# Differential attention: the two score products in turn on the two row halves of the array, and a mask that VectorE writes

## The chip, the cores and the metric

The kernel runs on one core of a Trainium2 chip. The metric is device time in microseconds of one execution, the median of three runs. Four compute engines matter here: TensorE multiplies matrices (PE in the profile; its weight loads are listed apart, as PEld), VectorE (DVE) and ScalarE (ACT) work on elements, GpSimd (POOL) does small things. DMAs bring the weights from memory.

## The reference, cut to what matters

The reference is a network of two layers and a last block, on 256 tokens of width 1024. A layer is a feed-forward part, a mixer and another feed-forward part. The mixer has three branches, and one of them is differential attention with 8 heads. A head has two sets of queries and keys of 64 features each; each set gives a softmax, and the second one times a learned lambda is subtracted from the first:

```python
sc = jnp.einsum('bqhmd,bkhmd->bhmqk', qblk, k).astype(jnp.float32) * scale   # m: the two parts
allowed = kchunk[None, :] <= (qp // CHUNK)[:, None]                          # chunks of 64 keys
p = jax.nn.softmax(jnp.where(allowed, sc, -jnp.inf), axis=-1)
w = p[:, :, 0] - lam_full * p[:, :, 1]
```

A query sees the keys of its own chunk of 64 and of the earlier ones. With query blocks of 128 that leaves one forbidden square in each block: the first 64 queries of a block against the last 64 of the keys that the block looks at.

## The kernel before, in words

All activations stay on the chip, and the weights (some 420 MB) stream through it once. A weight tile of 512 KB is loaded, split by ScalarE and VectorE into a high and a low part (`split`, lines 257 and 258), and multiplied as three products (lines 252 to 254, and 295 to 298). A list of items holds the weight tiles in order. After each tile, every active chain of other work (attention, state space and so on) is advanced by one stage, so the short products of the chains stand between the long streams of the weight products. The queues of the engines are in order; a scheduler at build time sets the order of the instructions and puts in the semaphores.

The chain of differential attention is `diff`. It is a software pipeline over the 8 heads with four stages: `s1` makes scores and softmax of a head, `s2` transposes the weights `p`, `s3` multiplies by the values, `s4` transposes the outputs. One step of the pipeline runs `s1` of head h, `s4` of h - 3, `s2` of h - 1 and `s3` of h - 2, in this order, and then waits for two weight tiles. There are 8 heads in each of two layers, so `s1` runs 16 times.

In `s1` the queries and keys of part m lie on partitions 64 m to 64 m + 63, so part 0 uses the upper half of the array's rows and part 1 the lower half. For each part, one PSUM bank `x[m]` takes the scores of both query blocks: columns 0 to 127 for block 0, columns 128 to 383 for block 1. Each score product (lines 753 and 755) is in float32, which runs as two passes. Behind each stands a product of one row in bf16 (lines 754 and 756) that adds a row with -1e30 in its first 64 entries, so that the first 64 queries lose the last 64 keys. VectorE then takes the maxima (757 and 758) and scales them (759), ScalarE the exponentials with their sums (763 and 765), VectorE the reciprocals, and the two parts are joined into `p` (771 and 772).

The array is used in three shapes around `s1`: all 128 rows in the weight products and transposes, 64 rows in the score products, and one row in the mask products.

Of the kernel before, what the change touches and what calls it, by code (L numbers as in the profile page):

```python
# [26 lines left out]
# order of the weight tiles and of the chains of work in the mixer and in the second block  # L27
# [3 lines left out]
# chains whose instructions come first where there is a choice  # L31
PRIO = {'narrow': 300, 'rope2': 300}
# leading weight tiles that are split ahead, in scratch of the chains
SPARE, SPARE2 = (1, 2), (1,)
# steps of the substitution that other work may follow
# [3 lines left out]
# 2 pi in parts of 8 bits (and a rest), so that products with 16-bit counts are exact  # L39
# [8 lines left out]
NEG = -1.0e30  # L48

# column offsets of the segments of w_mix_in  # L50
C_QA, C_KA, C_VA, C_Z, C_XBC, C_DT, C_QC, C_KC, C_VC, C_G = (
    0, 1024, 2048, 3072, 4096, 5632, 5648, 6672, 7696, 8720)
# column offsets in the table of constants
# [26 lines left out]
# [128, a, b] in tiles of 512 columns  # L80
# [9 lines left out]
class Net:  # L90
# [31 lines left out]
    # the constants that the first matrix products don't need  # L122
    def setup1(self):
        nc, I, T = self.nc, self.I, self.ctab
        nc.sync.dma_start(T[:, 128:384], I["ctab"][:, 128:384])
        T2 = self.t8([128, 1, 640], F32, "ctab2")[:, 0, :]
# [6 lines left out]
        nc.vector.tensor_copy(B[:, 128:384], T2[:, 384:640])  # L133
        nc.vector.tensor_copy(B[:, 384:512], T[:, 0:128])
        self.m_str, self.m_cau, self.m_chk, self.identb = (B[:, o:o + 128] for o in (0, 128, 256, 384))
# [3 lines left out]
        self.oneb = B[0:1, 512:576]  # L139
        nc.vector.memset(self.oneb, 1.0)  # L140
# [25 lines left out]
    # scratch of a chain; `prv` for scratch of the evacuation of projections  # L166
# [17 lines left out]
    # ---- order of work: a list of weight tiles and of things to do; chains advance one stage per weight tile  # L184
# [45 lines left out]
    # weight block [128, a, b] -> exact split into hi + lo  # L230
    def wload(self, src, a, b, spare=False):
        n = a * b
# [5 lines left out]
        if spare:  # L238
            # in scratch of the chains
            hi, lo = ([self.s2.tile([128, 512], F32R, name=i, tag="sc") for _ in range(2)] for i in ("hi", "lo"))  # L240
            for i in range(2):
                self.split(hi[i], lo[i], raw[:, i * 512:i * 512 + 512])
            return Rows(hi, b), Rows(lo, b)
# [5 lines left out]
    # three exact products hi*hi + hi*lo + lo*hi  # L249
# [19 lines left out]
    # the same for several columns: scalar engine, and one step of Newton's  # L269
# [17 lines left out]
    # ys[n] += (a^T)[tokens]^T @ W ; stationary a^T, moving W  # L287
# [13 lines left out]
    # [128 tok, n] per token block; fn(ps0, ps1)  # L301
# [32 lines left out]
    # [128 f, 2, 256 tok] of 256 columns; fn(ps)  # L334
# [21 lines left out]
    # 16 columns, token-major [128 tok, 2, 16] for the chain fn(pd)  # L356
# [20 lines left out]
    # token-major output of 1024 columns over kt tiles of a^T; the last tiles block by block; fn(tb, ys)  # L377
# [35 lines left out]
    # residual, layer norm, transposition: new x, x^T  # L413
# [40 lines left out]
    # one token block of x^T as hi, lo [128, 8, 256]  # L454
# [12 lines left out]
    def ffn(self, S_, w_in, w_out, g, b, mod=False, first=False):  # L467
# [12 lines left out]
        # first 256 columns token-major, so that they can start on the first token block  # L480
# [74 lines left out]
    # vectors of a layer, as columns or on every partition  # L555
    def columns(self, l, L):
# [29 lines left out]
        # lambda of the differential attention  # L586
# [128 lines left out]
    # rotary embedding of 4 heads (two parts each) and transposition  # L715
# [26 lines left out]
    # differential attention, one head a stage  # L742
    def diff(self, L):
# [3 lines left out]
        def s1(h):  # L747
            qT, kT = L["qa"], L["ka"]
            x = [self.bank([128, 384]) for _ in range(2)]
            mx = self.small.tile([128, 4], F32, name="mx", tag="mx")  # L750
            for m in range(2):
                p = slice(64 * m, 64 * m + 64)
                nc.tensor.matmul(x[m][:, 128:384], qT[p, h, 128:256], kT[p, h, :], start=True, stop=False)
                nc.tensor.matmul(x[m][:, 320:384], self.m_chk[0:1, :], self.oneb, start=False, stop=True)
                nc.tensor.matmul(x[m][:, 0:128], qT[p, h, 0:128], kT[p, h, 0:128], start=True, stop=False)
                nc.tensor.matmul(x[m][:, 64:128], self.m_chk[0:1, :], self.oneb, start=False, stop=True)
                nc.vector.tensor_reduce(mx[:, m:m + 1], x[m][:, 0:128], axis=AX.X, op=ALU.max)
                nc.vector.tensor_reduce(mx[:, 2 + m:3 + m], x[m][:, 128:384], axis=AX.X, op=ALU.max)
# [49 lines left out]
    # stages of n items, in a software pipeline; `rest` weight tiles for each step  # L808
# [10 lines left out]
    # softplus of a small [128, n] tile, accurate to float32 for small results too  # L819
# [18 lines left out]
    # step sizes and cumulated decays of the state-space branch  # L838
    def steps(self, L, pd):
# [21 lines left out]
        # the cumulated decays of every head as rows, hi and lo (first, second, second block)  # L861
# [7 lines left out]
    # causal convolution and twice the silu of 256 channels  # L869
# [93 lines left out]
    # stick-breaking attention, two heads of one parity a stage  # L963
    def stick(self, L):
# [5 lines left out]
        def s1(t):  # L970
# [11 lines left out]
            for nm, z in (("B", flat(B)), ("A", flat(A))):  # L982
# [3 lines left out]
                if t == 0 and nm == "B":  # L986
                    # one table for both exp and ln
                    self.tc.keep_in_program_order(nc.scalar.preload_act_table_set("natural_log_exp_and_others"))
# [48 lines left out]
    # vectors of the second block  # L1037
# [35 lines left out]
    # gain * cos and gain * sin of the rotary angles of the given positions, for q and k  # L1073
# [35 lines left out]
    # adaptive modulation: shift, gain, gate (twice) as rows of a DRAM tile  # L1109
    def modulation(self):  # L1110
# [3 lines left out]
        for s in range(6):  # L1114
# [11 lines left out]
            # sums over the partitions, as rows: quarter j on the partitions from 32 j  # L1126
# [20 lines left out]
    # two rows of the modulation on every partition  # L1147
# [7 lines left out]
    # modulated rms norm of one token block; out(n): where half n goes  # L1155
# [23 lines left out]
    def block2(self, S_, us):  # L1179
# [14 lines left out]
        # hi and lo of the two halves of the merged heads, transposed  # L1194
# [53 lines left out]
    # causal convolution and twice the silu of 256 channels  # L1248
# [15 lines left out]
    # decays and step sizes of the delta rule  # L1264
# [29 lines left out]
    # sums of squares over the heads of [128 f, 4, 256 tok], as [128 tok, 2, 8]  # L1294
# [12 lines left out]
    # queries, attention (transposed) and values of the delta rule  # L1307
    def gdn_qv(self, B):
# [5 lines left out]
        # what the squared norms of the queries make of the constant in the norm of the outputs  # L1314
# [25 lines left out]
    def gdn(self, B):  # L1340
# [4 lines left out]
        # values times step size, and decayed keys of the first chunk  # L1345
# [7 lines left out]
        # inverse norms of the keys  # L1353
# [23 lines left out]
        # decay, M (transposed) and attention (transposed); index tb * 8 + parity * 4 + i, head 2 i + parity  # L1377
# [28 lines left out]
    def chunk0(self, B, Xt):  # L1406
# [4 lines left out]
        # chunk 0  # L1411
# [18 lines left out]
    # outputs of one chunk, and their transposes  # L1430
# [62 lines left out]
    # transposed inverses of the 16 unit lower triangular I + M: blocks of 16 by substitution, one in each  # L1493
    # partition; then by doubling the block size
    def inverse(self, B, MT, Xt):
# [9 lines left out]
        # [(g, b, j), i, x, m] = M_m[i, j] of block (g, b) where x = b, transposed to [(g, x, m), i, b, j]  # L1505
# [11 lines left out]
        # Z[c, j] = inverse[j, c]  # L1517
# [28 lines left out]
        # levels and quarters, those of the first chunk ahead  # L1546
# [10 lines left out]
        # the last level needs just the quarter of M below the diagonal  # L1557
# [41 lines left out]
        # the inverses themselves; of the last level's input only the first quarter  # L1599
# [19 lines left out]
    # rotated heads of one token block, normalized unless the inverse norms (times 1 / 8) are to go to `out`  # L1619
# [103 lines left out]
    # gate, residual and modulated norm of the second half; then the experts  # L1723
    def gated(self, S_, B):
# [7 lines left out]
        def head():  # L1732
            # the router takes x: its weights times the gain, and the products of the shift
# [13 lines left out]
        def fn(tb, ys):  # L1747
# [19 lines left out]
            # column 8 p + k goes to k, p  # L1767
# [9 lines left out]
    # weights of an expert: gate and up for rows 8 p + k as [128, k, 2, 256], down for rows 2 p + k as [128, k, 1024]  # L1777
# [29 lines left out]
    # the same for the expert with the rows `idx`; beyond the last row nothing is read  # L1807
# [17 lines left out]
    # tokens of one block as hi + lo  # L1825
# [9 lines left out]
    # choice of experts: combine weights, places in the experts' slots and in the extra units  # L1835
    def route(self, B):
# [13 lines left out]
        # per token block and group  # L1850
# [4 lines left out]
        # one-hots of the first maximum and of the second among the 8 of every group; of the first group  # L1855
# [37 lines left out]
        # one-hots over all experts, and their places: rank among the expert's tokens, 0 where there is none  # L1893
# [17 lines left out]
        # weights of both choices  # L1911
# [16 lines left out]
        # units beyond the first 64 tokens of an expert  # L1928
        def rest():
# [14 lines left out]
            # which expert a unit belongs to; 32 where none  # L1944
# [360 lines left out]
```

## Time and profile before

| | |
|---|---|
| median of 3 runs | 2203.24 us (2202.16 to 2209.62) |
| span of the profiled execution | 2200.1 us (no other time of that execution is listed; the timed runs lie 2.1 us and more above it) |
| TensorE busy | 2142.3 us, 97% of the span |
| VectorE, ScalarE busy | 1346.7 us (61%), 994.9 us (45%) |
| DMA | 428.93 MB, 195 GB/s in the mean |
| the 16 runs of `s1` | 365 to 453 us (layer 0), 1219 to 1305 us (layer 1) |

Times in the rows are microseconds from the start of the span. A matrix product's row begins with its start; its end is modelled, so what the engine can do is read from one start to the next. A product that waits for its weights is listed from the start of the load. In a timeline, neighbouring instructions of one line are merged into one row with a count, and the second number is the time from the first start to the last end.

### The profile page before, as it was taken

To read this page: it belongs to the slowest core of one execution; us is meant where nothing else is said; L and a number is where in the kernel's file an instruction comes from. 1 tells how busy PE (TensorE), PEld (TensorE's weight loads), DVE (VectorE), ACT (ScalarE), POOL (GpSimd) and SP (SyncE) were. 2 spreads that over 40 slices of the span, in tenths; PEclk is the share of its full clock that TensorE was granted. 3 is DMA by queue.
4 is the path that set the end of the run, shared out by engine and by line. 5 is a ranking of instruction groups with operands and counts; after the bars stand their busy time and mean duration, and the time that the engine had idled before them with its cause. 6 is when DMAs were issued, how large, how long until landed. Compare 5 with 4: busy or idle time off the path is not lost.

```text
span 2200.1 us, 35342 instructions
## 1 busy us (share of the span) xinstructions
PE 2142.3 (97%) x14123; PEld 1821.5 (83%) x14123; DVE 1346.7 (61%) x2258; ACT 994.9 (45%) x1671; POOL 83.0 (4%) x73
## 2 busy tenths in 40 slices
PE   8999999999999999999999999999999899799998
PEld 8997987899999987998888789998998788544543
DVE  5556567765676667666677775567554895732232
ACT  5443554664554443444465565544443555211111
POOL 0000000100000000000000010000000021101000
PEclk9999999999999999999999999999999999899999
DMA  7665534444466786888543345555666423799996
GB/s 237 182 209 174 172 108 115 134 140 150 148 201 220 233 267 210 265 271 262 169 135 107 115 126 153 154 171 175 187 219 189 131 81 111 263 344 330 357 340 244
DMA packets 316984, 428.93 MB, mean 195 GB/s; under 512 B 20782, under 2 KB 262672, under 8 KB 315792
## 3 DMA queue, kind: packets, MB, share of 16 engines
q1 hardware_dynamic: 316384, 423.48, 61.5%
q8 instruction: 113, 1.85, 0.4%
q0 software_dynamic: 432, 3.15, 0.3%
q14 instruction: 55, 0.45, 0.1%
HBM read 425.50 MB, written 1.07 MB: 194 GB/s over the span
## 4 chain that ended last, share of the span: by engine, by line
PE 86%; DVE 6%; DMA 4%; ACT 1%; issue 1%; POOL 0%; SPq 0%; DVEq 0%; ACTq 0%; POOLq 0%
PE ps L252 14%; PE ps L254 14%; PE ps L253 14%; PE ps L1983 5%; PE y L295 4%; PE y L296 4%; PE ps L295 3%; PE ps L298 3%; PE ps L296 3%; PE y L298 3%; PE ps L2025 3%; DMA raw<-in_w_ada_dram 3%; PE y L284 1%; PE y L2038 1%; DVE lo L258 1%; PE ps L2130 1%
## 5 line engine op out<-in xcount | busy, mean ns | idle before, releaser
L258 DVE TENSOR_TENSOR lo<-raw,hi 128x1024 fp32r<-128x1024 f32 (+1 forms) x556 | 662.2, 1196 | 442.3 <-ACT hi L257 439.8
L257 ACT CAST hi<-raw 128x1024 fp32r<-128x1024 f32 (+1 forms) x556 | 568.8, 1028 | 711.2 <-PE ps L253 264.8
L254 PE MATMUL ps<-xh,lo 128*128 128x256 f32 (+1 forms) x2232 | 633.3, 284 | 3.5 <-DVE lo L258 3.5
L252 PE MATMUL ps<-xh,hi 128*128 128x256 f32 (+1 forms) x2232 | 636.6, 285 | 0.0
L253 PE MATMUL ps<-xl,hi 128*128 128x256 f32 (+1 forms) x2232 | 633.2, 284 | 0.0
L254 PEld LDWEIGHTS ps<-xh,lo 128*128 128x128 f32 (+1 forms) x2232 | 427.3, 191 | 4.4 <-DVE lo L258 3.7
L252 PEld LDWEIGHTS ps<-xh,hi 128*128 128x128 f32 (+1 forms) x2232 | 427.5, 192 | 2.4 <-issue 1.6
L253 PEld LDWEIGHTS ps<-xl,hi 128*128 128x128 f32 (+1 forms) x2232 | 427.4, 192 | 0.6
L295 PE MATMUL ps<-hi,xh 128*128 128x512 f32 (+1 forms) x368 | 147.1, 401 | 1.2 <-ACT xh L257 0.7
L298 PE MATMUL ps<-hi,xl 128*128 128x512 f32 (+1 forms) x368 | 144.6, 393 | 0.8 <-DVE xl L258 0.6
L296 PE MATMUL ps<-lo,xh 128*128 128x512 f32 (+1 forms) x368 | 144.2, 392 | 0.0
L295 PE MATMUL y<-hi,hh 128*128 128x512 f32 x352 | 137.5, 391 | 0.0
L296 PE MATMUL y<-lo,hh 128*128 128x512 f32 x352 | 137.0, 389 | 0.0
L1983 PE MATMUL ps<-wgu,hi 128*64 128x512 f32 x512 | 125.2, 601 | 0.0
L298 PE MATMUL y<-hi,hl 128*128 128x512 f32 x352 | 104.6, 389 | 0.0
L1983 PEld LDWEIGHTS ps<-wgu,hi 128*64 128x64 f32 x512 | 42.6, 139 | 71.0 <-issue 68.6
L1124 DVE SCALAR_TENSOR_TENSOR macc<-raw,cols,macc 128x1024 f32<-128x1024 f32 x42 | 53.9, 1284 | 57.0 <-DMA raw<-in_w_ada_dram 56.7
L295 PEld LDWEIGHTS ps<-hi,xh 128*128 128x128 f32 x368 | 70.5, 191 | 17.7 <-issue 2.0
L298 PEld LDWEIGHTS ps<-hi,xl 128*128 128x128 f32 x368 | 70.2, 191 | 17.2 <-DVE xl L258 2.7
L296 PEld LDWEIGHTS ps<-lo,xh 128*128 128x128 f32 x368 | 70.2, 191 | 13.1
L295 PEld LDWEIGHTS y<-hi,hh 128*128 128x128 f32 x352 | 66.1, 188 | 14.2 <-issue 0.8
L298 PEld LDWEIGHTS y<-hi,hl 128*128 128x128 f32 x352 | 66.1, 188 | 13.8
(607 smaller groups left out, 3248.7 us busy)
## 6 DMA issues: line engine op xcount, KB each, us to landing
raw<-in_w_mix_in_dram SPq DMA_DIRECT2D x184, 512.0 KB
raw<-in_ffn_w_in_dram SPq DMA_DIRECT2D x176, 512.0 KB
raw<-in_ffn_w_out_dram SPq DMA_DIRECT2D x88, 512.0 KB
wgu<-in_w_gate_dram SPq DMA_DIRECT2D x64, 512.0 KB
wgu<-in_w_up_dram SPq DMA_DIRECT2D x64, 512.0 KB
lo<-in_w_down_dram SPq DMA_DIRECT2D x54, 512.0 KB
raw<-in_w_branch_dram SPq DMA_DIRECT2D x48, 512.0 KB
raw<-in_w_ada_dram SPq DMA_DIRECT2D x48, 512.0 KB
```

The source lines that it names most:

```text
L252: mm(out, ah, bh, start=start, stop=False)
L253: mm(out, ah, bl, start=False, stop=False)
L254: mm(out, al, bh, start=False, stop=stop)
L257: self.nc.scalar.copy(hi, src)
L258: self.nc.vector.tensor_tensor(lo, src, hi.bitcast(F32), op=ALU.subtract)
L284: self.nc.tensor.transpose(pt[:, k, :], src[:, k * 128:(k + 1) * 128], self.ident)
L295: mm(y, ah[:, t], wh[:, c], start=start, stop=False)
L296: mm(y, ah[:, t], wl[:, c], start=False, stop=False)
L298: mm(y, al[:, t], wh[:, c], start=False, stop=stop)
L1124: nc.vector.scalar_tensor_tensor(acc, raw, c, acc, op0=ALU.mult, op1=ALU.add)
L1983: mm(gu[64 * e:64 * e + 64, c], u["x"](k)[:, 64 * e:64 * e + 64], w, start=k == 0 and i == 0, stop=k == KD - 1 and i == len(ws[0]) - 1)
L2025: mm(y[64 * e:64 * e + 64, :], u["hT"][:, k, 64 * e:64 * e + 64], wd[k][:, c], start=k == 0, stop=k == 1)
```

## The change

Both score products of query block 1 come first, part 0 and then part 1, and then both of block 0. The four mask products are gone. In their place VectorE writes -1e30 into the forbidden squares of each bank, both squares in one instruction (64 partitions, 2 x 64 columns), after the products and before the maxima. The bank's view grows from 384 to 512 columns so that the two squares lie at one stride (a bank holds 512 in any case). The table of constants loses the mask's row and its row of ones.

```diff
-            x = [self.bank([128, 384]) for _ in range(2)]
+            x = [self.bank([128, 512]) for _ in range(2)]
             mx = self.small.tile([128, 4], F32, name="mx", tag="mx")
+
+            for c, t, n in ((128, slice(128, 256), 256), (0, slice(0, 128), 128)):
+                for m in range(2):
+                    p = slice(64 * m, 64 * m + 64)
+                    nc.tensor.matmul(x[m][:, c:c + n], qT[p, h, t], kT[p, h, 0:n], start=True, stop=True)
             for m in range(2):
-                p = slice(64 * m, 64 * m + 64)
-                nc.tensor.matmul(x[m][:, 128:384], qT[p, h, 128:256], kT[p, h, :], start=True, stop=False)
-                nc.tensor.matmul(x[m][:, 320:384], self.m_chk[0:1, :], self.oneb, start=False, stop=True)
-                nc.tensor.matmul(x[m][:, 0:128], qT[p, h, 0:128], kT[p, h, 0:128], start=True, stop=False)
-                nc.tensor.matmul(x[m][:, 64:128], self.m_chk[0:1, :], self.oneb, start=False, stop=True)
+
+                nc.vector.memset(x[m][0:64, :].rearrange("p (a b) -> p a b", a=2)[:, :, 64:128], NEG)
                 nc.vector.tensor_reduce(mx[:, m:m + 1], x[m][:, 0:128], axis=AX.X, op=ALU.max)
                 nc.vector.tensor_reduce(mx[:, 2 + m:3 + m], x[m][:, 128:384], axis=AX.X, op=ALU.max)
...
-        nc.vector.tensor_copy(B[:, 128:384], T2[:, 384:640])
+        nc.vector.tensor_copy(B[:, 128:256], T2[:, 384:512])
...
-        self.oneb = B[0:1, 512:576]
-        nc.vector.memset(self.oneb, 1.0)
```

## Rows read from the trace of the kernel before

**Rows 1.** The page: busy times, and the chain that ended last.
```profile
PE 2142.3 (97%) x14123; PEld 1821.5 (83%) x14123; DVE 1346.7 (61%) x2258; ACT 994.9 (45%) x1671; POOL 83.0 (4%) x73
...
PE 86%; DVE 6%; DMA 4%; ACT 1%; issue 1%; POOL 0%; SPq 0%; DVEq 0%; ACTq 0%; POOLq 0%
```

**Rows 2.** Busy time by stretch: length, engines with counts, granted clock, DMA share, GB/s.
```profile
365.00:453.00 88.00, 88.00 (x547) 73.04 (x546) 68.23 (x172) 54.22 (x142) 7.68 (x6) 1.00 0.41 120
...
1219.00:1305.00 86.00, 86.00 (x487) 70.56 (x486) 62.18 (x155) 48.10 (x123) 6.14 (x5) 0.94 0.40 117
```

**Rows 3.** Timeline of PE around the first and last `s1`; count of one mask line.
```profile
365.20 0.70 PE L753 MATMUL y<-ka,qa 64*128 64x256 f32 x2
365.83 0.20 PE L754 MATMUL y<-bmask 1*128 1x64 bf16 x1
365.96 0.48 PE L755 MATMUL y<-ka,qa 64*128 64x128 f32 x2
366.37 0.20 PE L756 MATMUL y<-bmask 1*128 1x64 bf16 x1
366.50 0.70 PE L753 MATMUL y<-ka,qa 64*128 64x256 f32 x2
...
367.80 0.50 PE L296 MATMUL ps<-lo,xh 128*128 128x512 f32 x1
...
1301.03 0.70 PE L753 MATMUL y<-ka,qa 64*128 64x256 f32 x2
...
1303.63 0.44 PE L284 MATMUL y<-ctab,oa 128*128 128x128 f32 x2
...
L756 PE MATMUL y<-bmask x32: 197/198/198, 366.4 to 1303.5; 1*128 1x64 bf16 x32
```

**Rows 4.** Timeline of PE: products of 64 rows that stay on one half.
```profile
1772.02 1.16 PE L1392 MATMUL y<-gkk 64*128 64x128 f32 x8
1773.10 0.38 PE L1388 MATMUL y<-ctab,gg 128*128 128x128 f32 x1
...
245.10 0.71 PE L977 MATMUL y<-qc,kc 64*128 64x128 f32 x4
245.65 1.03 PE L980 MATMUL y<-qc,kc 64*128 64x256 f32 x4
246.61 0.28 PE L981 MATMUL y<-bmask 128*128 128x256 bf16 x1
```

**Rows 5.** Timeline of PE: line 1327 takes one half and then the other.
```profile
1805.15 0.70 PE L1678 MATMUL y<-sqkT 64*128 64x256 f32 x2
1805.69 1.60 PE L1327 MATMUL y<-gqv,gkk 64*128 64x128 f32 x16
1807.22 0.50 PE L296 MATMUL ps<-lo,xh 128*128 128x512 f32 x1
```

**Rows 6.** Groups of VectorE by form: busy, mean ns, idle before.
```profile
L559 DVE MEMSET rows<- 128x128 f32 x2 | 0.3, 165 | 0.0
L757 DVE TENSOR_REDUCE mx<-y 128x1 f32<-128x128 f32 x32 | 9.3, 291 | 14.3 <-PE y L756 14.1
```

**Rows 7.** Waits in 360 to 453: us, times, longest.
```profile
ACT hi L257 <- PE ps L253: 7.9, 8, 1.5
```

**Rows 8.** Timeline of VectorE and PE: head 2 of layer 0, then head 7.
```profile
391.43 0.75 DVE L772 SCALAR_TENSOR_TENSOR p<-p,sm 128x128 f32<-128x128 f32 x2
...
395.05 0.49 PE L284 MATMUL y<-ctab,p 128*128 128x128 f32 x3
...
450.45 0.74 DVE L772 SCALAR_TENSOR_TENSOR p<-p,sm 128x128 f32<-128x128 f32 x2
...
451.53 0.49 PE L284 MATMUL y<-ctab,p 128*128 128x128 f32 x3
```

**Rows 9.** Low clock in layer 1, one stretch of three, behind PE's row ahead.
```profile
1230.30 0.20 PE L756 MATMUL y<-bmask 1*128 1x64 bf16 x1
...
1231.05:1234.45 3.40, 3.40 (x19) 3.40 (x17) 0.87 (x3) 1.46 (x7) 0.00 (x0) 0.50 0.28 98
```

More of the change, by code (lines that the diff above doesn't have):

```diff
@@ L132, in setup1 @@
         nc.vector.tensor_copy(B[:, 0:128], T2[:, 256:384])
-        nc.vector.tensor_copy(B[:, 128:384], T2[:, 384:640])
+        nc.vector.tensor_copy(B[:, 128:256], T2[:, 384:512])
         nc.vector.tensor_copy(B[:, 384:512], T[:, 0:128])
-        self.m_str, self.m_cau, self.m_chk, self.identb = (B[:, o:o + 128] for o in (0, 128, 256, 384))
+        self.m_str, self.m_cau, self.identb = (B[:, o:o + 128] for o in (0, 128, 384))
         nc.vector.tensor_copy(B[:, 576:704], self.U)
```

## The prediction

> **What bounds the kernel now.** I read the page first: TensorE is busy for 97% of the span, and 86% of the chain that ended last is its work [rows 1]. A busy share can hide waits, so next the busy times by stretch, for the two stretches in which `s1` runs: TensorE is busy for all 88.00 of 88.00 us and all 86.00 of 86.00 us there, DMA for 0.41 of its time, ScalarE for 54 us, VectorE for 68 us [rows 2]. There the path is TensorE's queue itself; what is taken out of it ends the run sooner, as long as the products behind it have their inputs. The engine to watch is VectorE, at 68.23 of 88 us.
>
> Then the timeline of the score products. One head's `s1` begins at 365.20 and the next product at 367.80, so it holds the queue for 2.60 us; the last one holds it from 1301.03 to 1303.63, the same, and 32 mask products of line 756, two to a head, make 16 heads [rows 3]: 41.6 us in all. From start to start, a part is 0.63 us for the two passes of 256 columns (365.20 to 365.83), 0.13 for a mask product, 0.41 for the two passes of 128, 0.13 for a mask product; and the same again for part 1.
>
> **What a pass and a change of shape cost.** Line 1392 makes eight passes of 64 rows and 128 columns on one half in a row: 1772.02 to 1773.10, 1.08 us [rows 4]. Two of them alone take 0.41. Six passes more cost 0.67, so a pass of 128 columns costs u = 0.112 us, and entering and leaving such a run costs 0.41 - 0.22 = 0.19 us: a first load that nothing hides, and the wait at the end before a product of another shape. The pair of 256 columns gives v = (0.63 - 0.19)/2 = 0.22 for a pass. A check: line 977 and line 980, four passes of each width without a change between, should take 0.19 + 0.45 + 0.87 = 1.51; they take 245.10 to 246.61, 1.51 [rows 4]. So a head before is four passes of 256 and four of 128 (1.32 us), four times 0.19 (0.76), and four mask products (0.52): 2.60.
>
> **The change, step by step.**
>
> *The mask products go, and with them the changes of shape.* Four times 0.13 goes, and of four entries and exits one stays, 3 x 0.19 = 0.57. Left is 1.32 + 0.19 = 1.51 us if the passes still run one after the other: 1.09 less a head, 17.4 us over 16.
>
> *The halves take turns.* Does a pass on the lower half run beside one on the upper? Line 1327 does both halves in turn, eight passes on one and eight on the other. With line 1678 ahead of it, 18 passes run from 1805.15 to 1807.22, 2.07 us [rows 5]; one after another they would take 0.19 + 0.44 + 16 x 0.112 = 2.42. So 0.35 us, three passes, ran beside others. The second half begins when three passes of the first are still to come, and then both stream at full rate. In the new order a half never has more than two passes before the other half's turn, so here the two halves can run beside each other nearly throughout: half of 1.32, and 0.19, which is 0.85 us; if the lower half starts one load later (the 0.19 less an exit of some 0.08), 0.96. I take the middle, 0.90: 1.70 less a head, 27.2 us over 16. The ends are 1.51 (nothing side by side) and 0.85.
>
> The Trainium skill has a rule that speaks against this: "TensorE: Matmul & The Clock Gate", in the section on packing small matmuls ("The mechanism"), says that products start and end strictly in program order. By that rule a head would take 1.07 us and 24.5 us would be saved in all. The rows speak against it: strict order could hide one pass of line 1327 at the change of halves, and three are hidden [rows 5].
>
> *VectorE's two writes a head.* The trace has no write of a constant into PSUM. From below, the 128 x 128 MEMSET in SBUF takes 165 ns; from above, the maximum over 128 columns of the same bank, 291 ns [rows 6]. I take 0.2 us, nearer to the first, since the operation is the same: 32 x 0.2 = 6.4 us of VectorE's time, 3.2 in each stretch (2.6 to 4.7). By itself it lies beside the weight products that TensorE has queued behind the scores. The instruction waits for the products in its bank, as the maximum did; behind it in VectorE's queue stand the maxima and the splits of weights. The splits have room: ScalarE's half of the split waited 8 times for the weight products to give their buffers back [rows 7], so it runs as far ahead as the buffers let it.
>
> *The chain from maxima to `p`.* It must be over when the next step transposes `p`. For head 2, VectorE ends `p` at 391.43 + 0.75 = 392.18 and the transposes start at 395.05, 2.9 us later; for head 7, the last, it ends at 451.19 and they start at 451.53, 0.3 us later [rows 8]. Between a head's start and its transposes lie two runs of `s1`, so the transposes come 3.4 us sooner (1.7 for the last head). The chain gains too: both banks are complete about 1 us after the head's start, where part 1 took 2.6, less 0.4 for the two writes: about 1.2 us. The room falls from 2.9 to 2.9 - 3.4 + 1.2 = 0.7 us, and for the last head from 0.3 to about -0.2. And VectorE has 68 + 3 = 71 us of work in a stretch that shrinks from 88 to 74. So some of the gain comes back as waits for `p`: I put 0.2 us on each of 15 steps, 3 us (0 to 10).
>
> *The clock.* In layer 1 the granted clock is 0.94 over the stretch [rows 2], from three pieces of 3.4 us at half the full clock (1.2 in place of 2.4 GHz). The first begins at 1231.05, 0.6 us after the last mask product of an `s1` group (1230.30 and 0.13 for the product) [rows 9], and the other two follow such a group alike; layer 0, with the same groups, has none. Such a piece costs half its length, 1.7 us, 5.1 together. The new group has less dead time, so I expect two of the three to go, 3.4 us; other pieces may come or go as everything moves. Ends: 0 and 5.1.
>
> *The smaller constants* are made while the first layer streams, and cost nothing that ends late.
>
> **The sum.** The profiled span is 2200.1 us, and the median of the timed runs is 3.1 above it; I carry that over. -27.2 (products) + 3.0 (waits for `p`) - 3.4 (clock) = -27.6: a span of 2172.5, and a time of 2175.6 us.
>
> **The rivals.**
>
> *The halves don't overlap.* The 64-row passes run in series, without drains. For it: the overlap is shown for passes of 128 columns only, and at one change of halves. Against it: nothing else distinguishes the passes. -17.4 - 3.4 + 1 = -20, 2183 us.
>
> *The passes keep their order.* If a pass never starts before the one ahead of it in the program, only neighbours of different halves run together: three widths of 0.22 and two of 0.112 in series, and 0.19, is 1.07 us; 16 x 1.53 = 24.5 less, and 2203.2 - 24.5 - 3.4 + 3.0 = 2178 us. (This is the skill's rule above.) The three hidden passes speak against it.
>
> *VectorE takes over in the two stretches.* 71 of 74 us leaves it no room for its own waits. For it: in-order queues and 0.7 us of room for `p`. Against it: weight splits are far ahead, and the busy time counts an overlap of neighbours. If 10 us come back, 2203.2 - 27.2 - 3.4 + 13 = 2186 us.
>
> *Each change of halves costs like a change of shape.* Then all four pairs keep their 0.19 and only the masks go: 0.52 x 16 = 8.3 us, 2195 us. Rows 5 argue against it.
>
> *The change does nothing for the time:* what leaves the queue returns as waits; 2203 us. A queue without a gap speaks against it.
>
> *Slower: the write into PSUM is dear.* One mechanism: a write of 64 partitions in two pieces that takes VectorE 2 us and not 0.2. VectorE then needs 68 + 16 x 2 = 100 us in a stretch of 88, TensorE waits for `p` in every step, and each layer loses about 8 to 12 us net of what its own waits left free: about 2219 us. It decides from (88 - 68)/16 = 1.2 us a write on. Against it stand 165 and 291 ns [rows 6].
>
> **How the numbers follow.** Overlap with most of the gain kept: 0.57, 2176 us, by itself from 2169 to 2182. Kept order: 0.05. Series: 0.13. VectorE takes over: 0.14. Drains at each change: 0.05. Nothing: 0.02. Slower: 0.04. A measurement of this kernel tells about 0.3%, 6.6 us, from no change; so faster is the first four and part of the fifth, 0.91; same 0.05; slower 0.04. The range is 2167 to 2190: its lower end is 0.85 us a head, all three clock pieces gone, no waits (-28 - 5.1 is 2170) and 3 us for clock pieces elsewhere; the upper end takes in the cases at 2178, 2183 and 2186 with 4 us to spare.
>
> **What would show it.** In the profile after, one head from its first score product to the next other product: 0.85 to 0.96 us if the halves overlap, 1.5 if they run in series, 2.1 if each change drains. MEMSET rows on the score banks near 0.2 us. In the waits of TensorE, transposes of `p` waiting for line 772's successor: some tenths at most on a step; more than 0.7 on each would be VectorE taking over. The granted clock in layer 1's stretch above 0.94. A head of 1.07 us would show the kept order. The prediction is wrong if a head takes over 1.2 us or if TensorE's idle time in the two stretches passes 8 us.

## The result, and the profile after

| | before | after |
|---|---|---|
| median of the timed runs | 2202.7 us (2201.84 to 2209.62, 4 runs) | 2175.21 us (2174.6 to 2176.39, 4 runs) |
| span of the profiled execution | 2200.1 us | 2173.1 us (its own time 2174.99) |
| TensorE busy | 2142.3 us | 2113.4 us |
| VectorE busy | 1346.7 us | 1342.6 us |

The ratio is 0.9876, with a 95% interval of 0.9855 to 0.9897: the kernel became faster, by 27.5 us in the medians. The forecast was 2175.6 us.

The first two lines of the page after, busy times and the chain, answer to [rows 1]. TensorE is still what bounds the kernel, with the same share of a shorter span.

```profile
PE 2113.4 (97%) x14059; PEld 1805.8 (83%) x14059; DVE 1342.6 (62%) x2289; ACT 994.7 (46%) x1671; POOL 83.3 (4%) x73
...
PE 85%; DVE 7%; DMA 4%; ACT 2%; issue 1%; POOL 0%; SPq 0%; ACTq 0%; DVEq 0%; POOLq 0%
```

The busy times of the two stretches after, in the columns of [rows 2]. The stretch of layer 0 is 75 us long where it was 88, that of layer 1 about 73 where it was 86. TensorE's queue now has 1.3 us of gaps in each. VectorE has 65 of 75 us, and the granted clock of layer 1 is 1.00 where it was 0.94.

```profile
365.00:440.00 75.00, 73.69 (x506) 65.15 (x505) 65.29 (x181) 50.46 (x133) 8.19 (x6) 1.00 0.47 141
1206.00:1279.20 73.20, 71.89 (x492) 63.39 (x491) 64.30 (x178) 48.80 (x129) 6.98 (x6) 1.00 0.48 144
```

TensorE's timeline after, the first two runs of `s1`, answers to [rows 3]. The eight passes of a head are now one row, since nothing stands between them. From their start to that of the next product it is 366.30 - 365.44 = 0.86 us, where it was 2.60. The second head has the one gap of its layer that follows a group at once: 373.28 - 371.76 = 1.52 us, of which the bracket shows 0.60 of waiting for `p`.

```profile
365.44 0.92 PE L753 MATMUL y<-ka,qa 64*128 64x256 f32 x8
366.30 0.50 PE L294 MATMUL ps<-lo,xh 128*128 128x512 f32 x1
...
371.76 0.92 PE L753 MATMUL y<-ka,qa 64*128 64x256 f32 x8
373.28 0.30 PE L282 MATMUL y<-ctab,p 128*128 128x128 f32 x1 [0.60 <-DVE p L772]
```

VectorE's groups by form after, answering to [rows 6]: busy time, mean ns, idle before. The write into PSUM takes 165 ns, as the MEMSET in SBUF did, and the maxima behind it 277 ns.

```profile
L757 DVE TENSOR_REDUCE mx<-y 128x1 f32<-128x128 f32 x32 | 8.9, 277 | 0.0
L756 DVE MEMSET y<- 64x128 f32 x32 | 5.1, 165 | 1.3 <-PE y L753 0.8
```

TensorE's waits for `p` in the whole run after (us, times, longest; line 282 is line 284 of before, the transposes); the list of before has no such row.

```profile
PE y L282 <- DVE p L772: 2.6, 4, 0.7
```

**A measure for one stretch.** Total times of variants differ by a few us in parts of the run that no edit touches: the granted clock falls for pieces of 3.4 us and more at places that shift. So I also compare traces by place. Each product that no edit touches is paired with its like (same tiles and shape, same count from the start) in the first profile of before, and the median difference of start times is taken just ahead of a stretch (330 to 360 us, 1190 to 1215 us on the clock of before) and just behind it (490 to 500, 1330 to 1340). What it grows by is what the stretch gained or lost. The group sum is the time of the 16 runs of `s1` in TensorE's queue, from the first pass to the next product that is not a score or mask product; a wait at its end counts in it (1.2 of the 15.0 us after, so 13.8 without).

| kernel | group sum, us | layer 0, us | layer 1, us | time, us (ratio, 95% interval) |
|---|---|---|---|---|
| before | 41.68 | 0 | 0 | 2202.7 |
| before, second profile | 41.68 | +1.6 | -3.3 | 2202.27 (0.998 to 1.0011) |
| after | 15.0 | -11.5 | -16.2 | 2175.21 (0.9855 to 0.9897) |
| after, second profile | 15.0 | -11.5 | -16.2 | 2177.96 (0.9873 to 0.9911) |
| part by part | 15.1 | -12.0 | -16.7 | 2177.28 (0.9866 to 0.9898) |
| mask products kept | 22.8 | -9.4 | -14.1 | 2178.06 (0.9869 to 0.9901) |
| one half | 24.1 | -7.7 | -12.5 | 2174.7 (0.9864 to 0.99) |
| no mask | 13.7 | -11.7 | -16.4 | 2173.35 (0.9852 to 0.9885) |
| two writes | 20.0 | -9.2 | -13.6 | 2178.96 (0.9879 to 0.9912) |
| six writes | 24.5 | +2.3 | -3.4 | 2202.57 (0.998 to 1.0005) |
| late transposes | 15.0 | -12.3 | -17.0 | 2170.11 (0.9823 to 0.9875) |

(The ratio is to the kernel before on the same chip, whose medians lay between 2200.78 and 2203.11 us.) The two profiles of after agree to 0.1 us in both stretches. By the intervals, none of the variants from "part by part" to "two writes" can be told from the change itself; by the stretches they can.

### The profile page after: what moved, and what is told of

Its sections match the earlier page's. It is cut to its first block, busy times and chain, and to the rows that moved or that the text cites. A ratio compares the mean times of both kernels' runs of the same rounds, so it can differ in the third digit from the quotient of the medians.

```text
span 2173.1 us, 35223 instructions
## 1 busy us (share of the span) xinstructions
PE 2113.4 (97%) x14059; PEld 1805.8 (83%) x14059; DVE 1342.6 (62%) x2289; ACT 994.7 (46%) x1671; POOL 83.3 (4%) x73
## 3 DMA queue, kind: packets, MB, share of 16 engines
HBM read 425.50 MB, written 1.07 MB: 196 GB/s over the span
## 4 chain that ended last, share of the span: by engine, by line
PE 85%; DVE 7%; DMA 4%; ACT 2%; issue 1%; POOL 0%; SPq 0%; ACTq 0%; DVEq 0%; POOLq 0%
PE ps L250 14%; PE ps L252 14%; PE ps L251 14%; PE ps L1983 5%; PE y L293 4%; PE y L294 4%; PE ps L293 3%; PE y L296 3%; PE ps L296 3%; PE ps L294 3%; PE ps L2025 3%; DMA raw<-in_w_ada_dram 2%; DVE lo L256 2%; PE y L2038 1%; PE ps L2130 1%; PE y L282 1%
## 5 line engine op out<-in xcount | busy, mean ns | idle before, releaser
L296 PEld LDWEIGHTS ps<-hi,xl 128*128 128x128 f32 x368 | 69.6, 189 | 16.4 <-DVE xl L256 2.3
L294 PEld LDWEIGHTS y<-lo,hh 128*128 128x128 f32 x352 | 66.1, 188 | 14.4 <-DVE lo L256 1.1
```

The source lines that it names most:

```text
L294: mm(y, ah[:, t], wl[:, c], start=False, stop=False)
L296: mm(y, al[:, t], wh[:, c], start=False, stop=stop)
```

## The experiments

**1. Part by part: the old order of the products.** My theory was that the halves run beside each other whenever both have passes in the queue, in whatever order these were written; the rival was the rule by which products start in program order.

```diff
-            for c, t, n in ((128, slice(128, 256), 256), (0, slice(0, 128), 128)):
-                for m in range(2):
-                    p = slice(64 * m, 64 * m + 64)
+            for m in range(2):
+                p = slice(64 * m, 64 * m + 64)
+                for c, t, n in ((128, slice(128, 256), 256), (0, slice(0, 128), 128)):
```

> The changed kernel, with the score products in the old order (both of part 0, then both of part 1) and VectorE's mask. Theory: the two row halves have queues of their own, and the second half begins as soon as no more than three passes of the first are to come; with four passes a half that is at once, so a head still takes 0.85 to 0.97 us and the run 2175 to 2177 us: the turns in the order are not what pays, the missing mask products are. Rival, strict program order of starts: only the last pass of part 0 runs beside part 1, a head takes about 1.4 us, the run 2184 us.

TensorE's timeline of this kernel, its first group: 366.10 - 365.24 = 0.86 us.

```profile
365.24 0.93 PE L753 MATMUL y<-ka,qa 64*128 64x256 f32 x8
366.10 0.50 PE L294 MATMUL ps<-lo,xh 128*128 128x512 f32 x1
```

Inside a group (medians over the 16), the starts lie 13, 307, 13, 202, 13, 96 and 13 ns apart: four pairs. In the program, as written and as built, the first product of part 1 (two passes) stands behind two products of part 0 (four passes), yet it starts 13 ns after the first pass of part 0. So for a set of this length the order written is not what gives the gain; without the mask products between them the old order does as well. For longer sets that is not shown: with eight passes on one half ahead of it, the second half of line 1327 began only when three of them were still to come [rows 5].

**2. Mask products kept, products in turn.** Each pair of score products is followed by its two one-row mask products; VectorE writes nothing.

```diff
-                    nc.tensor.matmul(x[m][:, c:c + n], qT[p, h, t], kT[p, h, 0:n], start=True, stop=True)
+                    nc.tensor.matmul(x[m][:, c:c + n], qT[p, h, t], kT[p, h, 0:n], start=True, stop=False)
+                for m in range(2):
+                    nc.tensor.matmul(x[m][:, c + n - 64:c + n], self.m_chk[0:1, :], self.oneb, start=False, stop=True)
...
-                nc.vector.memset(x[m][0:64, :].rearrange("p (a b) -> p a b", a=2)[:, :, 64:128], NEG)
```

> The score products in turn on the halves, but the four one-row mask products kept (two behind each pair) and no write by VectorE. Theory: each change of shape ends the overlap, so a head is 0.63 for the wide pair, 0.41 for the narrow pair and 0.16 to 0.26 for each pair of masks: 1.36 to 1.56 us, 17 to 20 us less than before, 2183 to 2186 us. Rival, the turns alone pay and the mask products are cheap: a head of 0.85 us and four times 0.03, 2177 us. Rival, the mask products stop everything and the halves share nothing between them: 2.3 us and more, 2198 us.

The first group in its timeline: 1.37 us to the next product.

```profile
366.21 0.70 PE L754 MATMUL y<-ka,qa 64*128 64x256 f32 x4
366.84 0.23 PE L756 MATMUL y<-bmask 1*128 1x64 bf16 x2
367.00 0.49 PE L754 MATMUL y<-ka,qa 64*128 64x128 f32 x4
367.42 0.23 PE L756 MATMUL y<-bmask 1*128 1x64 bf16 x2
367.58 0.50 PE L296 MATMUL ps<-lo,xh 128*128 128x512 f32 x1
```

Four passes in turn take 0.63 us, as long as two passes of one half did before [rows 3]. The group is 0.52 us longer than after. So of the 1.75 us that a head lost in TensorE's queue, 1.23 come with the halves in turn (which leave two changes of shape of four) and 0.52 with the mask products. At the end less is left: 16 x 0.52 is 8.3 us, but the two stretches together gain only 4.2 us less than after, and the time, 2178.06 us, lies below the 2183 to 2186 expected. TensorE's waits for VectorE in the stretches are 0.6 us here against 2.6, which is 2.0 of the difference; the other 2.1 are not placed.

**3. One half.** Both parts use the upper half of the rows (the queries and keys of part 0 stand in for those of part 1). The instructions and their order are those of the changed kernel.

```diff
-                    p = slice(64 * m, 64 * m + 64)
+                    p = slice(0, 64)
```

> The changed kernel with both parts read from the upper half of the rows, so that part 1's scores are those of part 0 (its output differs). Nothing can run side by side; shapes, widths and VectorE's work stay. Theory: a head takes 1.51 us in place of 0.85, the run 10.5 us more than the changed kernel, 2185 to 2186 us; of some 28 us, 17.4 are the mask products and their changes of shape and 10.5 the overlap. Rival, the overlap is worth little on this path because p comes late anyway: the run within 3 us of the changed kernel.

```profile
365.20 1.57 PE L753 MATMUL y<-ka,qa 64*128 64x256 f32 x8
366.71 0.50 PE L294 MATMUL ps<-lo,xh 128*128 128x512 f32 x1
```

The group takes 1.50 to 1.52 us, as the four and four passes of lines 977 and 980 do [rows 4], and the two stretches give 3.8 us less each. This is the cleanest of the tests, since nothing but the half differs: the turns are worth 0.65 us a head in TensorE's queue, 10.4 in all. The stretches lose 7.5 of it, chiefly since the 2.6 us of waits for `p` are gone here. The total time missed my expectation. Behind 1930 us, in the last block, this kernel gained 7 us that the others don't; it has less low clock there, and its other values may send tokens to other experts, which I did not look into. The total says nothing on the halves here.

**4. No mask.** VectorE's write is left out, so forbidden keys are seen.

> The changed kernel without VectorE's write, so nothing is masked (its output differs). Theory: the two writes cost VectorE 0.3 us a head beside TensorE's products, and only the four waits for p (2.6 us together) shrink, by 0.3 us each at most: 0.5 to 1.5 us less than the changed kernel. Rival, a write into PSUM is dear or the crowded VectorE is what holds TensorE: 5 us less or more.

The waits for `p` shrink to 0.2 us a layer and every group takes 0.853 to 0.855 us, yet the stretches gain only 0.2 us each over the change. In TensorE's waits other rows of VectorE stand in their place, which the changed kernel has not in these stretches:

```profile
PE y L282 <- DVE oa L794: 1.3, 4, 0.5
...
PE y L282 <- DVE qs L729: 1.0, 2, 0.5
```

So the waits were mostly passed on to other inputs of the transposes. What VectorE's two writes cost the end is a few tenths of a us a layer, less than the theory had (the scheduler moved some neighbouring products in this variant too).

**5 and 6. More writes.** Each write of the mask is done six times, then twice.

```diff
-                nc.vector.memset(x[m][0:64, :].rearrange("p (a b) -> p a b", a=2)[:, :, 64:128], NEG)
+                for _ in range(6):
+                    nc.vector.memset(x[m][0:64, :].rearrange("p (a b) -> p a b", a=2)[:, :, 64:128], NEG)
```

> The changed kernel with each VectorE write of the mask done six times in a row, so ten more writes a head and 160 in all; the rest is the same. By the changed kernel's trace a write takes 165 ns and starts some 130 ns after the one before it, so VectorE works 1.3 to 1.6 us longer a head in the two stretches, between the products that read the first bank and the reduces. Theory: VectorE had room at this point (0.47 of the stretch busy), so the product group stays at 0.85 us, and the additional time goes first into the slack of the waits for p (two a layer, 2.6 us in all); the delay of a head's p stands ahead of the transposes of the next step and shows as a longer wait there: 2185 us (2177 to 2192), and head groups that start further apart. Rival, VectorE hides it all: the same as the changed kernel, 2175 (2173 to 2177), and no wait for p of over 1 us. Rival, a write delays the chain by its own length every time: 16 x 1.45 = 23 us, 2198 (2195 to 2202), with a wait for p in every head.

None of the three had the time: 2202.57 us, the whole gain lost. Two things had changed, and only one was meant. The scheduler at build time counts the writes as work, and in 10 of the 16 heads it now puts other products between part 0's passes and part 1's: eight heads stand as two sets of four passes, and in two heads part 1 is parted once more. A half alone in the queue has nothing to run beside, and a head in two parts takes 0.85 us twice. The theory also began from a number read in the wrong column: 0.47 is the share of the DMAs in the stretch after, while VectorE works for 65.29 of its 75.00 us, 0.87. The timeline of the third head, with three other products between the parts, and three rows of TensorE's waits in the whole run:

```profile
381.05 0.92 PE L753 MATMUL y<-ka,qa 64*128 64x256 f32 x4
381.89 0.50 PE L294 MATMUL ps<-lo,xh 128*128 128x512 f32 x1
...
382.79 0.92 PE L753 MATMUL y<-ka,qa 64*128 64x256 f32 x4
383.64 0.50 PE L294 MATMUL ps<-lo,xh 128*128 128x512 f32 x1
```

```profile
PE ps L252 <- DVE lo L256: 10.7, 8, 2.3
...
PE y L753 <- DVE oal L260: 4.3, 2, 2.2
...
PE y L282 <- DVE p L773: 1.2, 4, 0.4
```

Over the two stretches it is 26.7 us behind the change (13.9 and 12.8). The split groups, without the waits in them, are 23.6 - 13.8 = 9.8 of it. Two pieces of low clock in layer 0 (3.4 us each at half the clock) cost half their length, 3.4, if no wait hides a part of that. Waits of TensorE for VectorE in the stretches are 12.5 us against 2.6, so 9.9; and they are not where I had looked. The weight products wait for the low part of their split (5.5 of the 10.7 us of that row lie in the two stretches), and the scores for a bank that VectorE had not yet emptied, while the waits for `p` became shorter. The other 3.6 us I can't place. To part the splits from the load I took a smaller dose.

> The changed kernel with each write of the mask done twice (32 more in all; with six of each, 160 more, it took 27 us more, of which 9.5 in product groups that the build's scheduler had split: part 0's two products, other work, part 1's two, 1.69 us in place of 0.85; the rest was waiting for VectorE). Here the scheduler splits 6 of the 16 groups. Theory: each additional write costs the end about what it did there, (27.4 - 9.5) / 160 = 0.11 us, so 32 x 0.11 = 3.6, and the splits 6 x 0.84 = 5.0: 2184 (2181 to 2187). Rival, VectorE has room for a first few and the price comes only beyond: 5.0 and nothing else, 2180 (2178 to 2181).

It took 2178.96 us, and both stretches together lost 2.3 + 2.6 = 4.9 us, which is the 20.0 - 15.0 us of the 6 split groups and nothing else. The rival was right: 32 more writes cost nothing that shows, 160 more came with some 10 us of waits. VectorE has room, and it ends.

**7 and 8. The same two kernels again, for the clock.**

> The kernel before once more, with nothing changed, for a second profile of it. In its first profile the granted clock fell to 0.5 three times in the second layer's stretch (about 1231, 1251 and 1272 us), in the changed kernel's not at all. Theory: the fall is tied to the old product groups with their one-row products (each fell within a microsecond of such a group), so it comes again at two or three of the same places, within 2 us. Rival, it is chance how these pieces lie: other places and another number in this stretch, none possible, and then the 5 us that the clock gave back in this stretch are not due to the change. Time 2201 to 2204 in either case.

The busy times of this second execution of before, by stretch and by piece of low clock, and TensorE's row ahead of the first piece:

```profile
365.00:453.00 88.00, 88.00 (x535) 73.25 (x534) 66.99 (x170) 52.77 (x140) 7.67 (x6) 0.98 0.38 119
414.00:417.40 3.40, 3.40 (x19) 3.40 (x18) 2.26 (x8) 1.70 (x8) 0.25 (x1) 0.50 0.26 92
1217.50:1299.00 81.50, 81.50 (x479) 66.62 (x479) 60.87 (x153) 47.87 (x123) 6.14 (x5) 0.98 0.39 121
1257.10:1260.50 3.40, 3.40 (x18) 3.40 (x17) 2.14 (x5) 2.02 (x10) 0.57 (x1) 0.50 0.11 36
```

```profile
413.60 0.20 PE L756 MATMUL y<-bmask 1*128 1x64 bf16 x1
413.73 0.44 PE L284 MATMUL y<-ctab,oa 128*128 128x128 f32 x2
```

Neither theory holds as written. Here one piece lies in layer 0's stretch and one in layer 1's, where the first profile had none and three [rows 2, 9]. But this one too begins 0.3 us after the last mask product of a group (413.73 to 414.00), and all five of the two profiles begin within 0.7 us of such an end. Which groups are followed by a piece differs between the two executions; that it is a group holds for all five. The piece of layer 0 makes that stretch 1.6 us longer than in the first profile, half of its 3.4.

> The changed kernel once more, with nothing changed, for a second profile. The kernel before showed five low-clock pieces in the two stretches of differential attention over two profiles, each of them beginning within 0.7 us after an old product group, though not after the same ones. Theory: such pieces need the old groups, so again none in the two stretches. Rival, chance alone: at the rate of before, 2.5 a profile, one to four. Time 2174 to 2177 in either case.

```profile
365.00:440.00 75.00, 73.69 (x507) 65.26 (x506) 65.54 (x180) 50.82 (x133) 7.58 (x6) 1.00 0.46 140
1206.00:1279.00 73.00, 71.69 (x487) 63.06 (x486) 64.18 (x176) 48.56 (x128) 7.48 (x5) 1.00 0.48 144
```

Again the clock is 1.00 in both stretches, and it is in every other variant but the one with six writes. That one has no old groups, and two pieces in layer 0's stretch: one begins at 422.74, behind waits of TensorE of 2.17 and 0.41 us (the second ends 1.1 us ahead of it), the other at 453.46, at the end of a wait of 2.23. So the theory that such pieces need the old groups doesn't hold as written: here waits of TensorE lie ahead of the pieces. And the one profile of the variant that keeps the mask products, in shorter groups, has no piece. (The median of these executions, 2177.96 us, lies 2.8 above the first one, with 51.2 us at half the clock in the profile against 44.4, all of it outside the two stretches.)

**9. Late transposes.** In one step of the pipeline, the transposes of `p` come last, behind the products with the values (the expectation calls these "the splits of p").

```diff
-        yield from self.pipe(8, (s1, s2, s3, s4), 2, order=(0, 3, 1, 2),
+        yield from self.pipe(8, (s1, s2, s3, s4), 2, order=(0, 3, 2, 1),
```

> The changed kernel with another order of the stages of heads in one step: products and mask of the new head, then the stage of the oldest head, then the splits of p, then the transposes of p, where the transposes came ahead of the splits. Nothing is left out. Theory: the transposes of head 1's step stand 0.6 to 0.7 us for p in each layer because they follow the short product group at once; with other products of 0.5 to 1.2 us between, the wait shrinks to under 0.2 us, and the time to 2174 (2172 to 2176), about 1 to 2 us less than the changed kernel. Rival, the wait is only passed on, from the transposes to what reads the transposed table: same as the changed kernel, 2175 to 2176, with new waits of like sum. Rival, the later transposes delay the table and then the products of the next stage in every head: 2180 (2178 to 2184).

TensorE's waits for `p` in this kernel, to be held against the 2.6 us above:

```profile
PE y L282 <- DVE p L772: 1.2, 2, 0.6
```

It took 2170.11 us, ratio 0.9849 (0.9823 to 0.9875). The stretches account for 1.6 us of it (0.8 each), the size that the theory had, but not by the wait that it named: that in the step of head 1 stays 0.6 us, and the one in the step of head 4 is gone. The time lies 1.9 us below the range expected. In the two profiled executions (2167.07 and 2174.99 us) 6.3 us are left outside the stretches, and this one has 27.3 us at the low clock where that of the change has 44.4; half of the difference is 8.5, so the clock is enough to explain them, but that it does is not shown.

**10 and 11. A kernel faster than both.** The stick-breaking attention makes its scores for two heads of the same half in one stage. Here a stage takes a pair on the two halves, each in a bank of its own. Its later products follow the new grouping; only the scores are shown.

```diff
-            for i in range(2):
-                r = 2 * (t // 2) + i
-                nc.tensor.matmul(B[:, i, :], kT[p, r, 128:256], qT[p, r, 128:256], start=False, stop=i == 1)
-            for i in range(2):
-                r = 2 * (t // 2) + i
-                nc.tensor.matmul(A[:, i, :], kT[p, r, 0:128], qT[p, r, :], start=i == 0, stop=False)
...
+            for c, a, q in ((0, slice(0, 128), slice(0, 256)), (256, slice(128, 256), slice(128, 256))):
+                for i in range(2):
+                    p = slice(64 * i, 64 * i + 64)
+                    nc.tensor.matmul(X[i][:, c:c + q.stop - q.start], kT[p, t, a], qT[p, t, q], start=c == 0, stop=False)
```

> The changed kernel, and its idea carried to the other attention (stick-breaking): there a stage made the scores of two heads of one row half, all on that half; now it makes those of one pair on the two row halves in turn, each half in a bank of its own, 384 columns wide, with the mask still by products of an identity. Nothing is left out. Theory: passes on alternate halves lie beside each other as they do in the changed kernel, so the group, 1.51 us before with its masks, falls to 0.85 to 1.05 us, 8 groups a layer, 16 in all: 7 to 10 us less, of which the clock and waits give back 1 to 3: 2168 (2165 to 2171). Rival, the stage is bound by what follows (ScalarE's exp and softplus, VectorE's sums on 384 columns): same as the changed kernel, 2174 to 2176, with waits for these in place of products. Rival, the larger tiles cost more than the scores give back: 2178 to 2182.

TensorE's timeline of one stage, first in the changed kernel and then in this one:

```profile
259.39 0.28 PE L974 MATMUL y<-bmask 128*128 128x256 bf16 x1
259.61 0.71 PE L977 MATMUL y<-qc,kc 64*128 64x128 f32 x4
260.15 1.03 PE L980 MATMUL y<-qc,kc 64*128 64x256 f32 x4
261.11 0.28 PE L981 MATMUL y<-bmask 128*128 128x256 bf16 x1
261.15 0.47 PE L293 MATMUL ps<-hi,xh 128*128 128x512 f32 x1
```

```profile
258.94 0.92 PE L976 MATMUL y<-qc,kc 64*128 64x256 f32 x8
259.80 0.39 PE L978 MATMUL y<-bmask 128*128 128x256 bf16 x2
259.95 0.48 PE L293 MATMUL ps<-hi,xh 128*128 128x512 f32 x1
```

From 1.76 us it falls to 1.01 (the 1.51 of the expectation are without the masks). The time is 2163.76 us, ratio 0.9811 (0.9786 to 0.9837), a larger gain than expected. Counted by tile in TensorE's queue, the scores give 4.6 us a layer and their masks 0.6 to 0.8, as I had it. The products with the values give 4.4 more, which I had not counted: their pairs now alternate as well, between the two halves of the output partitions (128 rows and 64 columns of the array), and 11.7 us a layer became 7.3. A new gap of 0.8 us ahead of line 853 takes some of that back, and the products of the sums take 2.4 more, as there are more of them. The stretch gains 6.6 us a layer.

> Both edits that had beaten the changed kernel, in one: the stick-breaking scores by pairs on the two row halves, and the transposes of p behind the stage of the splits. Nothing is left out. Theory: they act at different places, so the parts add up. The first gave 13.0 us in the two stretches of stick-breaking (read from the offsets of equal products in the two traces), the second 1.6 us in the two stretches of differential attention; from 2175.2: 2160.6 (2157 to 2164, the width for where pieces of low clock fall). Rival, the second one's gain was only its lucky clock: 2163 to 2165, and no less waiting for p than in the kernel with the first edit alone.

With both edits the time is 2162.32 us (2158.06 to 2164.2), ratio 0.9816 (0.9796 to 0.9836). The stretches of differential attention again gain 0.8 us each and the waits for `p` are 1.3 us in place of 2.7, as the theory had it. But in the time it can't be told from the kernel of experiment 10: the two medians differ by 1.4 us, and their ranges cover each other.

## Why the prediction was right, step by step

**The products.** Forecast 27.2 us less, with 0.85 to 0.96 us a head and 0.90 chosen. Measured are 0.853 to 0.855 us in 14 of 16 heads, so 16 x (2.605 - 0.854) = 28.0. The lower end was right, half of the passes' time plus one 0.19: the lower half does not start a load later, but 6 to 7 ns after the upper one. One half alone takes 1.50 us in 14 of 16 heads where the sum had 1.51; both its terms, passes and changes of shape, stand.

**The strict order.** Starts of 13 ns apart for products that stand two behind in the program (experiment 1), and 0.86 us in place of 1.07, refute that rival. The Trainium skill, "TensorE: Matmul & The Clock Gate", in the section on packing small matmuls ("The mechanism"), says that products start and end strictly in program order. For two halves of the rows this case's traces show otherwise, and the measurement decides. The same goes, for TensorE's queue, for the sentence further up that the queues of the engines are in order.

**The mask products.** The sum had 0.13 us for each of four and 0.19 for each of three changes of shape. With the halves in turn (experiment 2) two mask products one behind the other take 0.16 us (366.84 to 367.00), and one change more than after remains: 2 x 0.16 + 0.19 = 0.51, measured 0.52. So the term for a change of shape holds a third time, and the one for a mask product is smaller where two stand together. The Trainium skill, "TensorEngine Tiling (Array Packing)", section "Key Properties", says that a change of tiling mode drains the array while tiles of one mode work in parallel. The trace agrees as far as it goes: 0.19 us for the one, and 6 to 7 ns between passes on the two halves. How much of the 0.19 is such a drain and how much the first load, no run here shows.

**VectorE's writes.** Forecast 0.2 us, measured 165 ns. That they lie beside other work held (experiments 4 and 6), and the rival by which VectorE takes over is not reached. It is a real mechanism all the same, and the prediction put its point too far off: 1.2 us a write, so 2.4 a head, from VectorE's room in the old stretch of 88 us. In the 75 us that the change leaves, VectorE has 75.0 - 65.3 = 9.7 us of room, 1.2 a head. Ten more writes, whose starts lie 0.14 us apart, are 1.4 us a head, and they came with waits of some 10 us.

**What comes back.** Forecast 3.0 us as waits for `p`, 0.2 on each of 15 steps. The sum was near and the picture wrong. There are two waits of 0.6 and 0.7 us in each layer, in the steps of heads 1 and 4, 2.6 in all, and none in the other steps: where the forecast expected the last head to be 0.2 us late, the scheduler had moved its transposes behind other products. Besides, each layer gives back some 1.3 us more, spread in tenths over weight products and transposes, whose order the scheduler had changed; where that comes from stays open.

**The clock.** Forecast 3.4 us, two of three pieces. All three went from layer 1's stretch, some 5 us (-16.2 there against -11.5 in layer 0, with the same groups). Part of it is the luck of the first profile: over two profiles of before it is 2.5 pieces a run, 4 us. Why these pieces went is not shown; less dead time in the group, the prediction's reason, was not tested by itself.

**The sum.** By the stretches it is -11.5 - 16.2 = -27.7, made of -28.0 for the products, +5.3 for what comes back (2.6 of it waits for `p`) and -5 for the clock; the rest of the run adds 0.7. The forecast was -27.6. Products, waits and clock were off by 0.8, 2.3 and 1.6 us, and the errors cancelled. The mechanism was right; that the time came out within 0.4 us was luck.

## What to carry to other kernels

Products that use half the rows should be queued in sets that hold both halves, with nothing of another shape between them: one set of eight passes here took half of its passes' time plus a single change of shape. Put the halves in turn where a set is longer, since no more than three passes of one half were seen to be overtaken (experiment 1 and [rows 5]). After such an edit, look at the built order as well as at the source, since a scheduler that counts costs may part the two halves again and give the gain away (1.69 us in place of 0.85). And judge variants by the stretch that the edit touches, with equal products paired between two traces: for the changed kernel it repeated to 0.1 us where the total time moved by 3. Where low-clock pieces fall into the stretch, as in the kernel before, it moved by 1.6 and 3.3 too, so the clock has to be read with it.

## What was not expected of the hardware

- Queue order did not hold passes on one half behind passes on the other: 13 ns between the first starts, with a second product of the first half between them in the program.
- The write of a constant into PSUM took the 165 ns of the one in SBUF, though in two pieces on 64 partitions.
- The pieces of low clock follow a kind of work closely (all five in the two stretches of the two profiles of before begin within 0.7 us of the end of an old group), but which of the 16 groups they follow differs between executions of one program.
